# A one-row early store between two loads of a streaming RMSNorm

## The chip, the cores and the metric

One core of one Trainium2 chip. The metric is device time in microseconds (us) of one execution; the median of several runs is quoted. Times drift a little from chip to chip and call to call, so kernels are compared within the rounds that they shared with the kernel before.

## The reference

```python
x = randn(16, 1024, 512) float32; gamma = ones(512) float32
rms = sqrt(mean(x ** 2, axis=-1, keepdims=True) + 1e-5)
return x / rms * gamma
```

That is 33.55 MB read and 33.55 MB written, with little arithmetic on each byte.

## The kernel before

The 16384 rows are four tiles of 128 partitions x 32 rows x 512 elements (8.4 MB each; one partition's share is 64 KB, contiguous in HBM, the main memory). Three slots in SBUF (the on-chip memory) hold tiles 0, 1 and 2; tile 3 reuses slot 0. Every load and every store of data is issued by SyncE, and the trace has all of their packets on one queue (q1 in the DMA view below) and the loads landing in the order of issue (tile 1 at 41.84 us, tile 2 at 62.83). "SyncE's ring" below is this queue: the transfers that SyncE has issued, waiting in order for the 16 DMA engines. A "turn" is a place in that order where loads are followed by a store.

```python
slots = [const.tile([P, R, D], fp32, name=f"slot{i}") for i in range(3)]   # R=32, D=512

def load(t, slot, r0, r1):
    nc.sync.dma_start(out=slots[slot][:, r0:r1], in_=xv[t][:, r0:r1])
def store(t, slot, r0, r1):
    nc.sync.dma_start(out=ov[t][:, r0:r1], in_=slots[slot][:, r0:r1])

load(0, 0, 0, 16)
load(0, 0, 16, 32)
load(1, 1, 0, 32)
load(2, 2, 0, 32)
# ... gamma is broadcast to all partitions ...

def compute(slot, r0, r1):
    for g in range(r0, r1, G):            # G = 8 rows
        # ... ScalarE squares (every other group with its own sum, else VectorE reduces from PSUM),
        # ... ScalarE sqrt, VectorE reciprocal
        for r in range(G):
            nc.vector.scalar_tensor_tensor(
                out=slots[slot][:, g + r, :], in0=slots[slot][:, g + r, :],
                scalar=rstd[:, r : r + 1], in1=gamma_b, op0=OP.mult, op1=OP.mult)

compute(0, 0, 32)
store(0, 0, 0, 32)
compute(1, 0, 16)
store(1, 1, 0, 16)
load(3, 0, 0, 16)
load(3, 0, 16, 32)
# ... compute and store of the rest of tile 1, of tile 2, of tile 3 in two halves ...
```

Of the kernel before, what the change touches and what calls it, by code (L numbers as in the profile page):

```python
# [1 line left out]

# [4 lines left out]


@with_exitstack
def kernel(  # L10
    ctx: ExitStack,
    tc: tile.TileContext,
    x: bass.AP,
    gamma: bass.AP,
    out: bass.AP,
):
    nc = tc.nc
    P = nc.NUM_PARTITIONS
    eps = 1e-5
    fp32 = mybir.dt.float32  # L20
    AF = mybir.ActivationFunctionType
    OP = mybir.AluOpType

    xf = x.flatten_outer_dims()
    of = out.flatten_outer_dims()
    N, D = xf.shape
    R = 32
    G = 8
    H = 4
    assert N == 4 * P * R  # L30

    xv = xf.rearrange("(t p r) d -> t p r d", p=P, r=R)
    ov = of.rearrange("(t p r) d -> t p r d", p=P, r=R)

    const = ctx.enter_context(tc.tile_pool(name="const", bufs=1))
    stats = ctx.enter_context(tc.tile_pool(name="stats", bufs=4))
    psum = ctx.enter_context(tc.tile_pool(name="psum", bufs=2, space=bass.MemoryType.PSUM))

    slots = [const.tile([P, R, D], fp32, name=f"slot{i}") for i in range(3)]
# [7 lines that stand above are left out]
    load(0, 0, 0, 16)  # L47
    load(0, 0, 16, 32)
    load(1, 1, 0, 32)
    load(2, 2, 0, 32)  # L50

    gamma_row = const.tile([1, D], fp32)
    nc.scalar.dma_start(out=gamma_row, in_=gamma.unsqueeze(0))
    ones_col = const.tile([1, P], fp32)
    nc.vector.memset(ones_col, 1.0)  # L55
    gamma_psum = psum.tile([P, H, D], fp32, name="sq")
    nc.tensor.matmul(gamma_psum[:, 0], ones_col, gamma_row, start=True, stop=True)  # L57
    gamma_b = const.tile([P, D], fp32)
    nc.vector.tensor_copy(out=gamma_b, in_=gamma_psum[:, 0])  # L59

    eps_t = const.tile([P, 1], fp32)
    nc.vector.memset(eps_t, eps)  # L62
    sq_scratch = const.tile([P, D], fp32)

    def compute(slot, r0, r1):
        for g in range(r0, r1, G):
            ss = stats.tile([P, G], fp32, name="ss")
            rms = stats.tile([P, G], fp32, name="rms")
            rstd = stats.tile([P, G], fp32, name="rstd")
            if (g // G) % 2:  # L70
                for h in range(0, G, H):
                    sq = psum.tile([P, H, D], fp32, name="sq")
                    nc.scalar.activation(out=sq, in_=slots[slot][:, g + h : g + h + H, :], func=AF.Square)  # L73
                    nc.vector.tensor_reduce(  # L74
                        out=ss[:, h : h + H], in_=sq, axis=mybir.AxisListType.X, op=OP.add
                    )
            else:
                for r in range(G):
                    nc.scalar.activation(  # L79
                        out=sq_scratch,  # L80
                        in_=slots[slot][:, g + r, :],
                        func=AF.Square,
                        accum_out=ss[:, r : r + 1],
                    )
            nc.scalar.activation(out=rms, in_=ss, func=AF.Sqrt, bias=eps_t, scale=1.0 / D)  # L85
            nc.vector.reciprocal(out=rstd, in_=rms)  # L86
            for r in range(G):
                nc.vector.scalar_tensor_tensor(  # L88
                    out=slots[slot][:, g + r, :],
                    in0=slots[slot][:, g + r, :],  # L90
                    scalar=rstd[:, r : r + 1],
                    in1=gamma_b,
                    op0=OP.mult,
                    op1=OP.mult,
                )

    compute(0, 0, 32)
    store(0, 0, 0, 32)
    compute(1, 0, 16)
    store(1, 1, 0, 16)  # L100
    load(3, 0, 0, 16)
    load(3, 0, 16, 32)
    compute(1, 16, 32)
    store(1, 1, 16, 32)
    compute(2, 0, 32)
    store(2, 2, 0, 32)
    compute(0, 0, 16)
    store(3, 0, 0, 16)
    compute(0, 16, 32)
    store(3, 0, 16, 32)  # L110


# [1 line left out]
_INS = ['x', 'gamma']  # L114
_OUTS = [((16, 1024, 512), 'float32')]


# [23 lines left out]
```

## Time and profile before

| | before |
|---|---|
| time, median (range) | 162.38 us (162.14 to 162.44) |
| span of the profiled run | 160.6 us |
| SyncE's DMA queue, share of 16 engines | 97.9% |
| VectorE busy | 77% |
| ScalarE busy | 50% |

From the DMA view of the kernel before (queue, kind: packets, MB, share of 16 engines' span):

```profile
q1 hardware_dynamic: 1728, 67.11, 97.9%
q14 instruction: 2, 0.02, 0.0%
```

The DMA engines are the bound and VectorE comes close behind. (The page's chain of the work that ended last runs through VectorE for 71% of the span.) The timeline (start us, us, engine) shows when SyncE issues its transfers:

```profile
0.73 1.95 SPq L42 DMA_DIRECT2D slot<-in_x_dram  x4
50.09 23.33 SPq L45 DMA_DIRECT2D out_dram<-slot  x2
...
145.80 2.07 DVE L88 SCALAR_TENSOR_TENSOR slot<-slot,rstd,gamma_b 128x512 f32<-128x512 f32 x3
147.90 0.33 SPq L45 DMA_DIRECT2D out_dram<-slot  x1
```

All four loads are in the ring by 2.7 us. The first store follows at 50.09 us, long before the loads have drained, and the last is issued when VectorE ends, near 147.9 us. Two waits from the waits view (who waited for whom: us in total, times, longest):

```profile
ACT sq_scratch L79 <- DMA slot<-in_x_dram: 12.6, 2, 10.3
ACT sq L73 <- DVE ss L74: 4.9, 1, 4.9
```

ScalarE waits for a load at the start and for tile 1 near 42 us; later in tile 1 it waits 4.9 us for VectorE.

The argument turns on a stretch of time in which the DMA engines are busy but move less. The windows view of the kernel before shows it; columns are the window, its length, busy time of each engine (with instruction counts), the clock, the DMA share and the GB/s:

```profile
22.50:37.00 14.50, 0.00 (x0) 0.00 (x0) 13.22 (x21) 10.79 (x22) 0.00 (x0) 1.00 1.00 434
37.00:42.20 5.20, 0.00 (x0) 0.00 (x0) 5.20 (x7) 0.64 (x2) 0.00 (x0) 1.00 0.93 403
57.00:62.80 5.80, 0.00 (x0) 0.00 (x0) 2.94 (x4) 5.58 (x18) 0.00 (x0) 1.00 1.06 362
107.00:112.80 5.80, 0.00 (x0) 0.00 (x0) 5.40 (x7) 1.75 (x4) 0.00 (x0) 1.00 1.00 429
```

A packet is long (2.4 us for 64 KB) and is counted whole, so single numbers of a short window wobble. Their ratio, GB/s divided by the share, wobbles less; it is the rate that the 16 engines together have while they are busy. It is 434 in the steady window and 403 / 0.93 = 433 at the end of load 1, but 362 / 1.06 = 342 around 58 us, where the ring turns from load 2 to the first store. The turn near 110 us, from load 3 to a store, gives 429 in this trace: no loss to speak of.

**The measure used below.** The trace has a record of each DMA packet. A 32 KB packet usually takes 1.213 us, a 64 KB packet 2.418. "Stretch" is what packets took beyond the usual time of their size, summed over the packets that started in a window and divided by 16, so it is us per engine. In the kernel before it is 1.33 us between 57 and 62.5 us, all of it in the last packet of load 2 on each of the 16 engines, which took 3.75 us on average (the prediction below says 3.77). The first packet of each engine, near 2 us, was stretched too, by 0.60 us on average here; the windows used below leave it out.

### The profile page before, as it was taken

To read this page: it belongs to the slowest core of one execution; us is meant where nothing else is said; L and a number is where in the kernel's file an instruction comes from. 1 tells how busy PE (TensorE), PEld (TensorE's weight loads), DVE (VectorE), ACT (ScalarE), POOL (GpSimd) and SP (SyncE) were. 2 spreads that over 40 slices of the span, in tenths; PEclk is the share of its full clock that TensorE was granted. 3 is DMA by queue.
4 is the path that set the end of the run, shared out by engine and by line. 5 is a ranking of instruction groups with operands and counts; after the bars stand their busy time and mean duration, and the time that the engine had idled before them with its cause. 6 is when DMAs were issued, how large, how long until landed. Compare 5 with 4: busy or idle time off the path is not lost.

```text
span 160.6 us, 402 instructions
## 1 busy us (share of the span) xinstructions
PE 2.0 (1%) x2; PEld 0.5 (0%) x2; DVE 123.4 (77%) x163; ACT 79.9 (50%) x162; POOL 0.2 (0%) x4
## 2 busy tenths in 40 slices
PE   4000000000000000000000000000000000000000
PEld 1000000000000000000000000000000000000000
DVE  0101909999999509999999999998999999998000
ACT  3008999930580999995099314003998960000000
POOL 0000000000000000000000000000000000000000
DMA  7999999969969997997999999999997997999993
GB/s 262 392 408 498 400 408 506 522 261 522 522 263 522 506 278 345 441 522 310 473 392 416 465 416 416 473 416 408 457 547 310 506 490 310 416 465 408 433 457 155
DMA packets 1732, 67.13 MB, mean 418 GB/s; under 512 B 193, under 2 KB 193, under 8 KB 194
## 3 DMA queue, kind: packets, MB, share of 16 engines
q1 hardware_dynamic: 1728, 67.11, 97.9%
q14 instruction: 2, 0.02, 0.0%
q10 hardware_dynamic: 2, 0.00, 0.0%
HBM read 33.56 MB, written 33.55 MB: 418 GB/s over the span
## 4 chain that ended last, share of the span: by engine, by line
DVE 71%; ACT 12%; DMA 8%; issue 1%; DVEq 0%
DVE slot L88 52%; DVE ss L74 18%; DMA slot<-in_x_dram 8%; ACT sq_scratch L79 6%; ACT sq L73 4%; DVE rstd L86 1%; ACT L85 1%; ACT rms L85 1%; DVEq L136 0%
## 5 line engine op out<-in xcount | busy, mean ns | idle before, releaser
L88 DVE SCALAR_TENSOR_TENSOR slot<-slot,rstd,gamma_b 128x512 f32<-128x512 f32 x128 | 85.7, 746 | 0.1
L79 ACT ACTIVATE sq_scratch<-slot 128x512 f32<-128x512 f32 x64 | 40.0, 625 | 13.9 <-DMA slot<-in_x_dram 12.6
L74 DVE TENSOR_REDUCE ss<-sq 128x4 f32<-128x2048 f32 x16 | 36.1, 2276 | 10.5 <-ACT sq L73 10.4
L73 ACT ACTIVATE sq<-slot 128x2048 f32<-128x2048 f32 x16 | 29.8, 1860 | 4.9 <-DVE ss L74 4.9
L85 ACT ACTIVATE rms<-ss,eps_t 128x8 f32<-128x8 f32 x16 | 4.4, 297 | 37.4 <-DVE ss L74 37.2
L79 ACT ACTIVATION_READ_ACCUMULATOR sq_scratch<-slot 128x1 f32 x64 | 11.9, 187 | 0.0
L86 DVE RECIPROCAL rstd<-rms 128x8 f32<-128x8 f32 x16 | 2.8, 188 | 9.8 <-ACT rms L85 9.8
L59 DVE COPY gamma_b<-sq 128x512 f32<-128x512 f32 x1 | 0.7, 692 | 3.2 <-PE sq L57 3.2
L57 PE MATMUL sq<-gamma_row,ones_col 1*128 1x512 f32 x2 | 2.0, 1122 | 2.2 <-DMA gamma_row<-in_gamma_dram 2.2
L79 ACT ACT_TABLE_LOAD x1 | 1.3, 1283 | 1.3 <-PEq L125 1.3
L85 ACT ACT_TABLE_LOAD x1 | 1.3, 1283 | 0.0
L55 DVE MEMSET ones_col<- 1x128 f32 x1 | 0.2, 165 | 0.8 <-PEq L125 0.8
L57 PEld LDWEIGHTS sq<-gamma_row,ones_col 1*128 1x128 f32 x2 | 0.5, 305 | 2.1 <-issue 2.1
L125 POOL MEMSET const-bfloat16-1.0<- 128x1 bf16 x1 | 0.1, 102 | 0.0
L125 POOL MEMSET const-uint8-127<- 128x1 uint8 x1 | 0.1, 102 | 0.0
L125 POOL MEMSET const-float32-0.0<- 128x1 f32 x1 | 0.1, 99 | 0.2 <-issue 0.2
L125 POOL MEMSET const-float32-1.0<- 128x1 f32 x1 | 0.1, 99 | 0.0
L62 DVE MEMSET eps_t<- 128x1 f32 x1 | 0.1, 59 | 0.0
## 6 DMA issues: line engine op xcount, KB each, us to landing
slot<-in_x_dram SPq DMA_DIRECT2D x4, 4096.0 KB, 19.3
out_dram<-slot SPq DMA_DIRECT2D x4, 4096.0 KB, 18.0
slot<-in_x_dram SPq DMA_DIRECT2D x2, 50.5
out_dram<-slot SPq DMA_DIRECT2D x2, 27.6
gamma_row<-in_gamma_dram ACTq DMA_DIRECT2D x1, 2.0 KB
```

The lines of the kernel that those rows point to most:

```text
L55: nc.vector.memset(ones_col, 1.0)
L57: nc.tensor.matmul(gamma_psum[:, 0], ones_col, gamma_row, start=True, stop=True)
L59: nc.vector.tensor_copy(out=gamma_b, in_=gamma_psum[:, 0])
L62: nc.vector.memset(eps_t, eps)
L73: nc.scalar.activation(out=sq, in_=slots[slot][:, g + h : g + h + H, :], func=AF.Square)
L74: nc.vector.tensor_reduce(out=ss[:, h : h + H], in_=sq, axis=mybir.AxisListType.X, op=OP.add)
L79: nc.scalar.activation(out=sq_scratch, in_=slots[slot][:, g + r, :], func=AF.Square, accum_out=ss[:, r : r + 1],)
L85: nc.scalar.activation(out=rms, in_=ss, func=AF.Sqrt, bias=eps_t, scale=1.0 / D)
L86: nc.vector.reciprocal(out=rstd, in_=rms)
L88: nc.vector.scalar_tensor_tensor(out=slots[slot][:, g + r, :], in0=slots[slot][:, g + r, :], scalar=rstd[:, r : r + 1], in1=gamma_b, op0=O ...
L125: nc = _bacc.Bacc("TRN2", target_bir_lowering=False, num_devices=1)
```

## The change

The intent, as far as the diff shows it: get a first small store into SyncE's ring early, between load 1 and load 2, at almost no cost in bytes, and send the other 31 rows of tile 0 when they are ready, as before.

```diff
     load(0, 0, 0, 16)
     load(0, 0, 16, 32)
     load(1, 1, 0, 32)
-    load(2, 2, 0, 32)
 ...
-    compute(0, 0, 32)
-    store(0, 0, 0, 32)
+    compute(0, 0, 8)
+    store(0, 0, 0, 1)
+    load(2, 2, 0, 32)
+    compute(0, 8, 32)
+    store(0, 0, 1, 32)
     compute(1, 0, 16)
```

## The prediction

> **What bounds the kernel now.** The DMA queue. The queue view gives the SyncE queue's packets 97.9% of 16 engines' span of 160.6 us (67.11 MB). In the trace's packet records 16 packets are in flight from 1.74 us to 159.2 us; engine idle time sums to only 0.4 us per engine. A 32 KB packet takes 1.213 us and a 64 KB packet 2.418 us, so a packet costs about 8 ns beside its bytes. VectorE, busy 123.4 us (77%), is the shadow limit: the timeline has its last multiply end at 147.9 us, the last store is issued then, and its first packet can start about 1.0 us later (as the first load's did: issued 0.73, first packet 1.74), just before the store ahead of it leaves the engines at about 149.2. So DMA leads VectorE at the end by about 0.3 us only.
>
> One more item: all 16 last packets of load 2 (57.9 to 58.7 us), those just before the first store packets, took 3.77 us on average in place of 2.42. That is 1.3 us in which every engine was slowed. The later load-to-store turn (near 110 us) and the store-to-load turn (near 91 us) show nothing like it, so I take it for a cost of the first store, not of each turn.
>
> **What the change moves.** No bytes are added. SyncE now waits, before load 2, for VectorE's first multiply of tile 0 (it starts at 24.1 us; 34.8 even if it waits for both first groups), then issues the row store and load 2. The Trainium skill, "DMA: Bandwidth & Descriptors", section "Anatomy of one DMA", says semaphore waits happen on the issuing sequencer, not in the DMA engines; "Queues, rings and completion order" says each engine consumes descriptors in ring order. The trace agrees: landings follow the order of issue. Tile 0 and load 1 keep the engines busy until about 41.5 us, so load 2 is issued 6 to 16 us before the ring runs dry: no bubble. The order on VectorE is unchanged; ScalarE moves one square of tile 2 by one place (0.8 us, against a wait of over 6 us).
>
> Cost: 128 extra packets, 8 per engine, about 8 ns each, estimated from the packet times above: +0.07 us, perhaps +0.15 with one more set of semaphore writes (9 ns each). The row store brings 0.6 us of traffic ahead of load 2, which lands near 63.5 us in place of 62.8; ScalarE starts tile 2 at 66.15, so that is covered.
>
> The 1.3 us first-store cost should move to the end of load 1 (near 41 us), not go away. Load 1 then lands near 43.2 in place of 41.84. ScalarE starts tile 1 later by as much, but it later waits 4.88 us for VectorE (the waits view), which absorbs it. Since DMA is saturated throughout, moving the stall wins nothing. If it did vanish, VectorE's end at 147.9 us would still limit the gain to about 0.3 us.
>
> **Prediction.** 162.5 us, 8 in 10 between 162.0 and 163.2. Faster by over 2%: 1%; within 2%: 97%; slower by over 2%: 2%.
>
> **What would show it.** DMA share still about 98%; SyncE issues load 2 near 25 us (35 at most) and it lands near 63.5; slowed packets at the end of load 1, none at the end of load 2; VectorE's last multiply still ends near 147.9; row packets of 2 KB near 0.1 us each.
>
> **What would make it wrong.** The stall occurring at both turns (+1.3 us, near 163.8); 2 KB writes at a 64 KB pitch being much slower than their bytes; the late issue of load 2 leaving a bubble near 41 us; a later landing of load 1 that VectorE does not absorb.

## The result

| | before | after |
|---|---|---|
| time, median (range) | 162.41 us (162.14 to 162.53, 4 runs) | 162.08 us (162.06 to 162.14, 4 runs) |
| ratio, 95% interval | | 0.9983 (0.9966 to 1.000) |
| span of the profiled run | 160.6 us | 160.3 us |

Ratios here are the mean time of one kernel's fast runs over that of the other's of the same rounds, so not quite the ratio of the medians quoted beside them. The difference is 0.33 us of medians, at the edge of what these runs resolve; a later repeat (e6) gave 0.9992 (0.9962 to 1.0022).

The same views of the kernel after. DMA queue:

```profile
q1 hardware_dynamic: 1872, 67.11, 97.9%
q14 instruction: 2, 0.02, 0.0%
```

Timeline:

```profile
0.73 1.33 SPq L42 DMA_DIRECT2D slot<-in_x_dram  x3
24.86 0.35 SPq L45 DMA_DIRECT2D out_dram<-slot  x1
25.25 0.43 SPq L42 DMA_DIRECT2D slot<-in_x_dram  x1
50.10 23.33 SPq L45 DMA_DIRECT2D out_dram<-slot  x2
...
145.82 2.07 DVE L87 SCALAR_TENSOR_TENSOR slot<-slot,rstd,gamma_b 128x512 f32<-128x512 f32 x3
147.92 0.33 SPq L45 DMA_DIRECT2D out_dram<-slot  x1
```

The bytes are the same, in 144 more packets (128 of the row, 16 that count up its semaphore). Load 2 is issued at 25.25 us, while load 1 still keeps the engines busy until about 41 us, and VectorE ends where it did. Waits:

```profile
ACT sq_scratch L78 <- DMA slot<-in_x_dram: 12.9, 2, 10.3
ACT sq L72 <- DVE ss L73: 4.6, 1, 4.6
```

Tile 1 came 0.3 us later, and ScalarE's later wait for VectorE took up exactly that. Windows:

```profile
22.50:37.00 14.50, 0.00 (x0) 0.00 (x0) 13.21 (x21) 10.80 (x22) 0.00 (x0) 1.00 1.00 434
37.00:42.20 5.20, 0.00 (x0) 0.00 (x0) 5.20 (x7) 0.30 (x1) 0.00 (x0) 1.00 0.97 388
57.00:62.80 5.80, 0.00 (x0) 0.00 (x0) 2.93 (x3) 5.58 (x18) 0.00 (x0) 1.00 0.99 379
107.00:112.80 5.80, 0.00 (x0) 0.00 (x0) 5.40 (x7) 1.74 (x4) 0.00 (x0) 1.00 1.02 441
```

The rate of a busy engine is now 388 / 0.97 = 400 at the end of load 1 (433 before) and 379 / 0.99 = 383 at the end of load 2 (342 before). The loss is split between both turns. In packet records: 0.31 us of stretch at load 1's end and 0.69 at load 2's, in sum 1.00 where it was 1.33.

**Which engine sets the time.** Within one engine a packet starts where the one before ended, so the records can be linked into 16 chains, one for each engine. The span ended 1.2 to 1.4 us after the last data packet in every trace, so the slowest engine sets it. In the kernel before the engines ended between 158.48 and 159.22 us (median 158.76); after, between 158.50 and 159.00 (median 158.58). The earliest ends did not move; their engines had to wait for the last store, issued at 147.9 us: 9 engines have an empty gap of over 0.04 us between 148.3 and 149.3 us after the change, but only 4 before. The slowest engine in both traces is one that had to carry an instruction fetch (the queue q14 above; 8 KB each, near 46 and 64 us): 0.31 us for the fetch's own packet, and a following packet 0.33 to 0.35 us too long. On this slowest engine the stretch at the two turns was 1.42 us before and 1.13 after, and its end moved by 0.22 us, most of the 0.3 us between the two spans. In all eleven traces whose chains close with the same number of packets of each large size on every engine (all but e4, e10 and e11), the slowest engine was one of the two so hit.

### The profile page after: what moved, and what is told of

Read it like the earlier page. It is cut to its first block, busy times and chain, and to the rows that moved or that the text cites. A ratio compares the mean times of both kernels' runs of the same rounds, so it can differ in the third digit from the quotient of the medians.

```text
span 160.3 us, 404 instructions
## 1 busy us (share of the span) xinstructions
PE 2.0 (1%) x2; PEld 0.5 (0%) x2; DVE 123.4 (77%) x163; ACT 79.9 (50%) x162; POOL 0.2 (0%) x4
## 3 DMA queue, kind: packets, MB, share of 16 engines
q1 hardware_dynamic: 1872, 67.11, 97.9%
## 4 chain that ended last, share of the span: by engine, by line
DVE 71%; ACT 12%; DMA 8%; issue 1%; DVEq 0%
DVE slot L87 52%; DVE ss L73 18%; DMA slot<-in_x_dram 8%; ACT sq_scratch L78 6%; ACT sq L72 4%; DVE rstd L85 1%; ACT L84 1%; ACT rms L84 1%; DVEq L138 0%
```

## The experiments

All kernels gave correct results. One table of stretches (us per engine) serves them all; "turn 1" is the end of load 1 (37 to 41.5 us), "turn 2" the end of load 2 (57 to 62.5 us).

| kernel | turn 1 | turn 2 | sum | time, median | ratio to before, 95% |
|---|---|---|---|---|---|
| before | 0.00 | 1.33 | 1.33 | 162.41 | 1 |
| e5, before again | 0.00 | 1.29 | 1.29 | 163.43, one run | |
| after | 0.31 | 0.69 | 1.00 | 162.08 | 0.9983 (0.9966 to 1.000) |
| e6, after again | 0.38 | 0.46 | 0.84 | 162.66 | 0.9992 (0.9962 to 1.0022) |
| e1, row behind load 2 | 0.00 | 1.09 | 1.09 | 162.62 | 1.0019 (0.9991 to 1.0048) |
| e2, row to scratch | 0.53 | 0.30 | 0.83 | 162.76 | 1.0021 (1.0006 to 1.0036) |
| e3, 32 KB halves | 0.01 | 0.80 | 0.81 | 162.72 | 1.0037 (1.0004 to 1.0071) |
| e4, row in load 0 | 0.21 (at 8 to 13 us) | 0.86 | 1.07 | 163.04 | 1.0034 (1.0019 to 1.0049) |
| e7, early start, before | 0.00 | 1.17 | 1.17 | 163.05 | 1.0013 (0.9988 to 1.0037) |
| e8, early start, after | 0.35 | 0.42 | 0.77 | 162.40 | 0.9972 (0.995 to 0.9994) |
| e9, eight rows | 1.35 | 0.00 | 1.35 | 162.83 | 1.0025 (1.0012 to 1.0039) |
| e11, early start, eight rows | 1.40 | 0.03 | 1.43 | 163.31 | 1.0053 (1.0034 to 1.0073) |
| e10, ladder of rows | 0.55 | 0.00 | 0.55 | 162.29 | 0.9988 (0.9973 to 1.0004) |
| e12, row by GpSimd | 0.00 | 1.16 | 1.16 | 162.45 | 0.9999 (0.9986 to 1.0012) |

In the calls of e1 to e4, e5 to e8 and e9 to e12, the kernel before took 162.43, 162.87 and 162.54 us. The traces and the times do not carry the same weight: a trace is one run, and times of one kernel vary by up to 1.5 us within a call (e3, e6). The turn near 110 us, clean in the kernel before, was not clean in every trace: between 105 and 114 us the stretch was 0.21 us in e7, 0.14 in e8, and 0.10 in e5 and in e6.

My theory after the result, FIRST: the first stores of a run carry a cost, once. Rivals: SIZE, the stretch is set by the sizes of the packets that meet at a turn; and later TURN, each turn at this place pays for itself.

### e1_row_late: the row split off, but not moved ahead of load 2

```diff
     load(2, 2, 0, 32)          # stays where it was before
 ...
-    store(0, 0, 0, 32)
+    store(0, 0, 0, 1)
+    store(0, 0, 1, 32)
```

> The row is split off tile 0 but its store stays behind load 2, so the only load-to-store turn of the first half is load 2 (64 KB packets) to row (2 KB packets) to rest (62 KB packets). I count the time by which the last packets of load 2 exceed 2.418 us, mean over the 16 engines (before: 1.34 us; after: 0.31 at the end of load 1 plus 0.69 at the end of load 2). Theory FIRST (one cost of the first stores of a run): about 1.3 us at the end of load 2, time as before, 162.4. Theory SIZE (the stretch is set by the size of the first store packets behind the last load packets, small for a row): about 0.3 us, DMA ends about 1 us earlier, but VectorE's end near 147.9 allows at most 0.3 us: 162.1.

The window of e1 at load 2's end:

```profile
57.00:62.80 5.80, 0.00 (x0) 0.00 (x0) 2.94 (x4) 5.58 (x18) 0.00 (x0) 1.00 1.10 387
```

Measured: 1.09 us of stretch at load 2's end (a rate of 387 / 1.10 = 352, where before had 342), time not distinguishable from before. SIZE falls: the packets behind the load's last packets are the same 2 KB ones as in the kernel after, where the stretch was 0.31. What differs is what stands behind the row in the ring: here 62 KB stores, there loads.

### e2_row_scratch: the same early row, to another tensor

```diff
-    store(0, 0, 0, 1)
+    nc.sync.dma_start(out=scratch[:, 0:D], in_=slots[0][:, 0, :])   # scratch: an HBM tensor, row pitch 128 KB
     load(2, 2, 0, 32)
 ...
-    store(0, 0, 1, 32)
+    store(0, 0, 0, 32)
```

> As after, but the row goes to a scratch tensor in HBM, not to the output, and tile 0 is then stored whole (64 KB packets); 0.26 MB more is written (+0.6 us of traffic). Theory FIRST-ANY (any earlier write takes part of the cost): 0.3 us excess at the end of load 1, 0.7 at the end of load 2, as after. Theory FIRST-REGION (the output's own memory must be touched): 0.3 us at load 1, 1.3 us at load 2. Theory SIZE: 0.3 and then 1.3, as the turn at load 2 has 64 KB packets on both sides as before; SIZE and FIRST-REGION are not told apart here. Time: DMA ends 0.3 us (FIRST-ANY) to 0.9 us (others) later than before, 162.7 to 163.3.

The windows of e2:

```profile
37.00:42.20 5.20, 0.00 (x0) 0.00 (x0) 5.20 (x8) 0.30 (x1) 0.00 (x0) 1.00 0.66 239
57.00:62.80 5.80, 0.00 (x0) 0.00 (x0) 2.84 (x3) 5.58 (x17) 0.00 (x0) 1.00 1.04 429
```

Measured: 0.53 and 0.30 (rates of 362 and 412). The second stretch fell from 1.33 to 0.30 although nothing had been written to the output before it, and although it has 64 KB packets on both sides as before. So the output's memory need not be touched, and this goes against SIZE once more. The time is 0.2% longer, for 0.26 MB more written.

### e3_halves: load 2 and store 0 in 32 KB packets

```diff
-    load(2, 2, 0, 32)
+    load(2, 2, 0, 16)
+    load(2, 2, 16, 32)
 ...
-    store(0, 0, 0, 32)
+    store(0, 0, 0, 16)
+    store(0, 0, 16, 32)
```

> The order of before, but load 2 and store 0 are each cut in two, so that the first load-to-store turn has 32 KB packets on both sides, as the turn near 110 us of before has, which showed no stretch. Theory SIZE: no stretch at the turn near 61 us (under 0.2 us), DMA ends about 1.2 us earlier, VectorE limits the gain to about 0.3 us: 162.1. Theory FIRST: about 1.3 us of stretch, spread over one or two 32 KB packets per engine; time as before, 162.4.

Measured: 0.80 us. SIZE expected under 0.2 and FIRST about 1.3; neither number is met. The cost does not need 64 KB packets; in this one trace it was smaller with 32 KB ones. The time was not better than before, though SIZE had expected 162.1 us.

### e4_prime_out: a row of zeros within load 0

```diff
+    prime = const.tile([P, D], fp32, name="prime")
+    nc.gpsimd.memset(prime, 0.0)
+    nc.sync.dma_start(out=ov[0][:, 0], in_=prime)   # the scheduler put it between load 0's halves
     load(0, 0, 0, 16)
     load(0, 0, 16, 32)
```

> A row of zeros per partition is stored to the output (overwritten later by the true row) between the two halves of load 0; everything else as before, with 0.26 MB more written (+0.6 us of traffic). Theory FIRST: the cost moves to the end of load 0's first half (near 11.5 us), 0.3 to 1.3 us there, and at most 0.7 us is left at load 2's end. Theory SIZE: near 0 at 11.5 us (32 KB load packets), and 1.3 us at load 2's end as before. Time 162.4 to 163.2 in either case, because 0.6 us of traffic is added and load 0's second half lands about 1 us later; the stretch is what tells the theories apart.

Measured: 0.21 us there and 0.86 left at load 2's end (FIRST had allowed 0.3 to 1.3 and at most 0.7). In this one trace a small store far from tile 0's own store still took part of the cost (0.86 us were left, where the three traces with the turn of before have 1.17 to 1.33). It did not take all of it.

### e5_before_again and e6_after_again: how stable is the stretch?

No edit in either.

> The kernel before, unchanged, for a second look at its packets. If the stretch at the first load-to-store turn is a fixed cost, the last packets of load 2 exceed 2.418 us by 1.2 to 1.5 us on average again; if it varies from run to run by as much as kernels differ (0.3 to 0.7 us), the differences so far between kernels say nothing.

> The changed kernel, unchanged, to tighten the interval of its time and for a second look. Fixed cost: 0.2 to 0.4 us at the end of load 1 and 0.6 to 0.8 us at the end of load 2, ratio 0.997 to 0.9995. Chance: other values, ratio about 1.000.

Measured: 1.29 in place of 1.33 for before, 0.38 and 0.46 in place of 0.31 and 0.69 for after. The full stretch of the kernel before repeats within 0.04 us (a third kernel with the same turn, e7, has 1.17); the second stretch of after varies by 0.2, which is smaller than its distance to before's, but 0.46 lies outside the 0.6 to 0.8 that a fixed cost was expected to give. The one run of e5 is slow in the end (163.43 us) for another reason: its slowest engine had a fetch, 1.63 us of stretch at load 2's end and a further 0.64 near 110 us, and ended at 160.31 us. The time of after could not be tightened: its six runs spread from 161.88 to 163.34 us.

### e7_fast_before and e8_fast_after: VectorE taken off the end

```diff
-    load(0, 0, 0, 16)
+    load(0, 0, 0, 8)
+    load(0, 0, 8, 16)
     load(0, 0, 16, 32)
```

once on before (e7) and once on after (e8).

> Before, with the first load cut again (rows 0 to 8 and 8 to 16), so that ScalarE and VectorE start about 4.5 us earlier and VectorE no longer limits the last store. If VectorE's end at 147.9 us were part of the bound, the time would fall; if the slowest DMA engine alone bounds before, the end stays at 159.2 and the time at 162.2 to 162.6. My theory (slowest engine: one that loses 0.6 us to an instruction fetch and 1.4 us to the stretch): 162.3.

> After, with the same earlier start. If the gain of the row store is about 0.35 us per engine of shorter stretch, of which VectorE's end hid a part on the 15 engines that are not the slowest, this kernel is 0.3 to 0.5 us faster than the fast-start version of before (161.8 to 162.0 against 162.3), and its engines end at 158.2 to 158.8. If the gain was chance, both are equal.

Measured in the same rounds: e7 163.05 us (162.75 to 163.45), e8 162.40 us (162.26 to 162.58); the ranges do not overlap. Both absolute forecasts (162.3, and 161.8 to 162.0) were missed, where before took 162.87; the forecast difference of 0.3 to 0.5 was exceeded. An earlier VectorE alone gains nothing, as expected, which fits a kernel before that is bound by its slowest DMA engine. With VectorE out of the way the row store is worth 0.65 us of medians (0.21 without, between before and e6), and e8 is 0.28% faster than before. Against after in the same call it is 0.26 us of medians faster, inside after's spread there. In e8's trace the first engine ended at 157.98 us and the median one near 158.3, below the 158.5 us at which VectorE's last store had held the engines of before and after. So part of the saved stretch had indeed been hidden behind VectorE on these engines. For the time this shows little, because the slowest engine sets it: in after's trace that engine was empty for only 0.05 us before the last store, and in e6's for no more than 0.04.

### e9_rows8 and e11_fast_rows8: a larger early store

```diff
-    store(0, 0, 0, 1)
+    store(0, 0, 0, 8)
     load(2, 2, 0, 32)
 ...
-    store(0, 0, 1, 32)
+    store(0, 0, 8, 32)
```

e9 on after, e11 on e8.

> As after, but eight rows (16 KB per partition) go out between load 1 and load 2, and 24 rows later. Stretch so far, at load 1's end and load 2's end: before 0 and 1.33 (again: 1.29), after 0.31 and 0.69 (again: 0.38 and 0.46). Theory FIRST (the first stores pay, each later turn pays less, the more has been written): 0.3 to 1.0 us at load 1's end, at most 0.3 us at load 2's end, sum 0.6 to 1.1. Rival TURN (every load-to-store turn at this place in the run pays by what stands behind it in the ring, a big store 1.2 us, a row 0.3 us because the loads return after it): about 1.2 at load 1's end and 0.5 to 0.7 at load 2's, sum over 1.7, slower than before. Time: FIRST 162.0 to 162.4 against 162.4 of before; TURN over 162.6.

> The eight early rows together with the earlier start of VectorE (load 0 cut in three), a candidate that may beat both kernels. The earlier-start version of after was 0.28% faster than before. FIRST: the same or a little better, ratio 0.995 to 0.998. TURN: worse than it, ratio 1.000 or more.

The windows of e9:

```profile
37.00:42.20 5.20, 0.00 (x0) 0.00 (x0) 5.20 (x7) 0.30 (x1) 0.00 (x0) 1.00 0.73 205
57.00:62.80 5.80, 0.00 (x0) 0.00 (x0) 2.97 (x4) 5.58 (x18) 0.00 (x0) 1.00 1.15 497
```

The rate of a busy engine is 205 / 0.73 = 281 at load 1's end and 497 / 1.15 = 432 at load 2's. The packets say 1.35 and 0.00 us. This is what the prediction had expected of a single row: the whole cost moves to turn 1, and turn 2, with 64 KB load packets and 48 KB store packets, is free. TURN's sum of over 1.7 us falls, and so does FIRST's hope of a sum below 1.1. Nothing is won, and both kernels are slower than before: 162.83 us for e9, and a ratio of 1.0053 for e11. On the times alone FIRST missed (162.0 to 162.4, and 0.995 to 0.998) and TURN's over 162.6 and 1.000 or more were met; it is the stretches that refute TURN. For e9 a new stretch of 0.19 us near 64 us is part of that; e11's last engine ended at 160.82 us, and I did not settle why it is the slowest of all.

### e10_ladder: four rows between quarters of load 2

```diff
     store(0, 0, 0, 1)
-    load(2, 2, 0, 32)
+    load(2, 2, 0, 8)
+    store(0, 0, 1, 2)
+    load(2, 2, 8, 16)
+    store(0, 0, 2, 3)
+    load(2, 2, 16, 24)
+    store(0, 0, 3, 4)
+    load(2, 2, 24, 32)
 ...
-    store(0, 0, 1, 32)
+    store(0, 0, 4, 32)
```

> Four row stores, each before a quarter of load 2 (16 KB packets), then the other 28 rows: five load-to-store turns in place of two. FIRST (a cost that is paid off by earlier writes): the turns' stretches fall from one to the next, the last one (before the big store) is under 0.3 us, and the sum stays at or under that of after (0.8 to 1.0 us). TURN (each turn pays its own price): 0.3 us at each row and 0.5 to 0.7 at the big store, sum 1.5 to 2 us, and the time 0.7 us or more above after's.

The windows of e10:

```profile
37.00:42.20 5.20, 0.00 (x0) 0.00 (x0) 5.20 (x6) 0.30 (x1) 0.00 (x0) 1.00 0.66 235
57.00:62.80 5.80, 0.00 (x0) 0.00 (x0) 3.04 (x4) 5.58 (x19) 0.00 (x0) 1.00 1.03 435
```

The rate is 235 / 0.66 = 356 at the first turn and 435 / 1.03 = 422 at the last. The packets say 0.55 us at the first of five turns, 0.03 at most in sum at the three in between, and 0.00 before the big store. TURN is refuted a second time, and the cost here is less than half of before's. The time, 0.9988, is no proof of a gain, and 11 engines of its trace have an empty gap of over 0.04 us near 148.5 us, waiting for the last store.

### e12_row_gpsimd: the row on another queue

```diff
     load(2, 2, 0, 32)          # stays where it was before
 ...
-    compute(0, 0, 32)
-    store(0, 0, 0, 32)
+    compute(0, 0, 8)
+    nc.gpsimd.dma_start(out=ov[0][:, 0:1], in_=slots[0][:, 0:1])
+    compute(0, 8, 32)
+    store(0, 0, 1, 32)
```

> The row store goes out on GpSimd's queue near 26 us, in the middle of load 1, and all loads of SyncE are issued at the start as before, so SyncE's ring has no turn at load 1's end. FIRST (any early write pays part of the cost): the stretch at load 2's end falls from 1.3 to 0.3 to 0.9 us. If the place of the row in SyncE's own ring matters, 1.2 to 1.4 us stay there. Time 162.0 to 162.4 in the first case, 162.4 to 162.7 in the second.

From e12's timeline, its DMA view (two lines) and its windows view:

```profile
25.10 0.67 POOL L98 DMA_DIRECT2D out_dram<-slot  x1 [24.65 <-DVE slot L88]
q0 software_dynamic: 80, 0.26, 0.4%
out_dram<-slot POOLq DMA_DIRECT2D x1, 256.0 KB, 17.3
57.00:62.80 5.80, 0.00 (x0) 0.00 (x0) 2.97 (x4) 5.58 (x18) 0.00 (x0) 1.00 1.00 345
```

The rate is 345 around load 2's end, and the stretch 1.16 us, close to the 1.2 to 1.4 expected if the row's place in SyncE's own ring matters and far from the 0.3 to 0.9 of "any early write". The Trainium skill, "DMA: Bandwidth & Descriptors", section "Issuing engines are not separate DMA queues", says that all issuing engines' transfers run on the same 16 engines and interleave. They did (the row, issued at 25.1 us, landed 17.3 us later, its packets scattered through load 1), but for this cost it was not the same as the row store of the kernel after. Which difference counts is not shown, because e12 changes three things at once: the queue, the packets (64 of 4 KB in place of 128 of 2 KB) and their place (one at a time between load packets from 29 to 40 us, not eight in a row on each engine at load 1's end).

## Why the prediction was right or wrong

- **The time.** 162.5 was forecast with a range of 162.0 to 163.2; 162.08 was measured. The class, within 2%, and the range held. The sign did not: I expected 0.1 us more, and the first rounds showed 0.33 us less. The range was no test of the step that failed below: by the prediction's own limit (VectorE's end) even a stall that vanished would have given about 162.1 us, inside the range too.
- **No bubble from the late load 2: right.** It was issued at 25.25 us and landed at 63.06 us (forecast 63.5; before 62.83). The Trainium skill, "DMA: Bandwidth & Descriptors", section "Anatomy of one DMA" (its heading names the path from GpSimd), puts semaphore waits on the issuing sequencer, and this trace of SyncE's transfers agrees: SyncE held the row until 24.86 us, just after VectorE's first multiply (24.11 us, 0.75 long), and issued load 2 0.04 us after the row's issue ended (24.86 + 0.35), while the DMA share in the window from 22.5 to 37 us was 1.00.
- **The price of the row's packets: right.** A 2 KB packet took 0.084 us where near 0.1 was expected; the 2 KB writes at a 64 KB pitch were not slow.
- **Later tile 1 absorbed by ScalarE's wait: right in kind.** Tile 1 landed at 42.18 us; 43.2 was forecast, because I had put the whole stretch there.
- **The step that failed:** "The 1.3 us first-store cost should move to the end of load 1 ..., not go away", and "none at the end of load 2". In the kernel after, 0.31 us moved there, 0.69 stayed at load 2's end and 0.33 us went away (e6: 0.38, 0.46 and, against e5, 0.45). That the cost is in the main paid once is well supported by e9, where the whole of it moves and turn 2 is free, and by e10, where four later turns are nearly free. The error was to take it as a fixed amount. A first store that is one row with loads behind it, at load 1's end, paid 0.31 to 0.55 us (after, e6, e8, e2, e10), and less than the rest was left to be paid.
- **VectorE as a limit of the gain: shown for most engines, not for the time.** With VectorE earlier, engines ended before 158.5 us, and the change was worth 0.65 us against 0.33 in the first rounds and 0.21. But e8 lies inside after's spread there, and the slowest engine, which sets the time, had at most 0.05 us to lose to VectorE in the two traces of after.
- **What I missed about the end.** I compared VectorE with "the DMA" as a whole and found a lead of 0.3 us. In the kernel before the 16 engines end up to 0.7 us apart, and the slowest, one that an instruction fetch held up by 0.6 us, sets the time.

**What stays open.** What the engines do during the stretch is not shown by any run; neither is why a row costs less than eight rows, nor why the sums differ (0.55 to 1.43 us). The data only say that a sum of 1.1 to 1.4 goes with a first store in SyncE's ring that has at least 16 KB per partition of stores in a row behind a load, and 0.55 to 1.1 with a first store of one row with a load behind it; e3, with 32 KB packets and 0.80, fits neither, and almost all of these kernels have one trace each, where two traces of one kernel differ by up to 0.2. That the first loads of every trace run slow as well (0.40 to 0.61 us in each engine's first packet) may or may not have to do with it; nothing here tests it. An early-start version of the ladder, the combination that these results suggest, was not run.

## What to carry to other kernels

When a kernel is bound by DMA, look at the packets around each turn from loads to stores, not at the share alone: here the engines were 97.9% "busy" in both kernels while 1.3 us of that before, and 1.0 after, was packets running slow at two turns. A cost that appears once is not thereby a constant: vary what comes first before reckoning that moving it gains nothing. And where a second engine runs 0.3 us behind the bound, take it out of the way before judging a small gain: here the gain stood clear of the spread (0.65 us, ranges apart) only then.

## What the Trainium skill lacked or had wrong

- "DMA: Bandwidth & Descriptors" does not mention that the last load packets before a ring's first store run slow: 1.33 us per engine in the kernel before (again 1.29), all of it in one packet each, in the main paid once per run (the later turn near 110 us took 0.21 us at most), and 0.55 us in the one trace with one-row stores mixed into the loads.
- The same page, "Issuing engines are not separate DMA queues", lacks that the same row store need not act alike from another issuing engine: the row in SyncE's ring left 0.69 and 0.46 us at load 2's end, the row on GpSimd's queue 1.16 us. Whether the ring itself matters, or the packets' size or place, is not shown.
- "Runtime: NRT & Kernel Launch", section "Instruction fetch mechanics", says of a crossed instruction block that its cost is mostly hidden. The sequencers did not visibly wait here either (the waits view of the kernel before puts only 2.1 and 0.2 us down to "issue", both at the start), but the data path did: each of two 8 KB fetches (0.309 us) took 0.5 to 0.7 us from the one DMA engine that carried it, and in eleven of eleven traces the slowest engine was one of the two.
